# Low weight parts behind narrow products, newest sums first, and a gate multiplication on VectorE, in a hybrid decoder block on one core

## The chip, the cores and the metric

The kernel runs on one core of a Trainium2 chip. The metric is the device time of one execution in microseconds. TensorE (PE in the views; PEld is its weight load), VectorE (DVE), ScalarE (ACT), GpSimd (POOL) and SyncE (SP, which issues the weight DMAs) work side by side, each through its own instruction queue, in the order of the program, and wait for each other by semaphores.

## The reference

One decoder layer over 256 tokens of width 2048 in float32: a SwiGLU feed-forward network (FFN) of width 5632, a mixer (differential attention, a causal convolution, two sigmoid gates), a second FFN, and a final norm.

```
def swiglu(h, w_gate, w_up, w_down):
    return (jax.nn.silu(h @ w_gate) * (h @ w_up)) @ w_down

x = x + 0.5 * swiglu(rms_norm(x, ffn1_norm_g[l]), ffn1_w_gate[l], ffn1_w_up[l], ffn1_w_down[l])
h = rms_norm(x, mix_norm_g[l])
z = h @ w_in[l]
q, k, v, glu_a, glu_b, gate_a, gate_c = jnp.split(z, splits, axis=-1)
...
merged = jax.nn.sigmoid(gate_a) * attn_branch + jax.nn.sigmoid(gate_c) * conv_branch
x = x + merged @ w_out[l]
x = x + 0.5 * swiglu(rms_norm(x, ffn2_norm_g[l]), ffn2_w_gate[l], ffn2_w_up[l], ffn2_w_down[l])
return rms_norm(x, final_norm_g)
```

## The kernel before

All large matrix products are made in a reduced float format from split operands: a float32 weight is the sum of a high part (`wh`, a copy rounded to the format) and a low part (`wl`, what the rounding left), and so is an activation. A product is high x high + high x low + low x high.

**Weights.** They come in units of 512 rows x 512 columns (1 MB, `KU` = 4 row tiles), in the order in which they are used, into three raw buffers. The class `Weights` splits each unit in two halves (`KH` = 2 row tiles): `high_to` issues the copy to `wh` on ScalarE (L94, six buffers), `low_to` the subtraction to `wl` on VectorE (L103, four buffers). When both low parts of a unit are issued, its raw buffer is given up and the DMA for the unit three further on is issued (L107, on SyncE). `next` is called once per half and hands out the two parts. It first runs `high_to` and `low_to` ahead, so the low parts of the next unit are issued where a unit begins. They wait until TensorE has used the buffers that they overwrite.

**Products.** `lin` makes 512 output columns for 256 tokens, in four column tiles `ct`, each in a PSUM bank of its own (five banks in rotation). For each unit there are 16 wide products (L331: high weights by the activation's high and low parts side by side, 512 columns) and 16 narrow ones (L335: low weights by the activation's high part, 256 columns). Even units run wide, then narrow; odd units, and the last one of a product, narrow, then wide. A product over 2048 rows has four units, so TensorE's list reads wide, narrow, narrow, wide, wide, and so on: stretches of 32 equal products, half from one unit and half from the next. While the last unit's wide products run, each finished column tile starts a flow, which takes it out of PSUM: `halves_sum` (a ScalarE copy `rh`, L392, and a VectorE addition, L394) and then what the product needs. In the FFN an `up` product multiplies by the gate (L424) and splits the result (L261 on ScalarE, L263 on VectorE); a `gate` product multiplies by `rstd` (L404, VectorE), applies Silu (L406, ScalarE) and multiplies by `rstd` again (L407, GpSimd). `lin_tok` is the other form of product, with the tokens as rows (L375 to L377).

**The order.** No scheduler decides it: the program is recorded as it is written. `tick` is called behind each column tile; it moves every open flow one step on and then the side jobs (attention, convolution, small loads), each at a rate of its own. A flow's `yield` ends a step.

**The start.** Nothing is loaded ahead, so the first product takes its first three units half by half (`halves`). Before each half, `start` makes two tiles of the normed activation `h` and issues the squares for the norm on GpSimd (L273, L275).

The FFN's `w_gate`, `w_up` and `w_down` are used in three groups of 4, 4 and 3 column blocks; each block is a `gate` and an `up` product.

Of the kernel before, what the change touches and what calls it, by code (L numbers as in the profile page):

```python
# [25 lines left out]
KU = 4  # L26
KH = 2
# [14 lines left out]
class Weights:  # L42
# [54 lines left out]
    def low_to(self, n):  # L97
        while self.nlow < min(n, len(self.units) * KU // KH):
# [6 lines left out]
            if k + KH == KU:  # L105
                del self.raw[u]
                self.load_to(u + 1 + self.raw_bufs)  # L107

    def next(self, held=0, early=True):


        i = self.i

        def ahead(bufs):
            n = i + bufs - held
            if self.extra and n > min(self.extra) and i <= max(self.extra):
                n = min(n + len(self.extra), max(self.extra) + 1 + bufs)
            return n

        if early:  # L120
            self.high_to(ahead(self.high_bufs))
        self.low_to(ahead(self.low_bufs))
        self.i += 1
        return self.highs.pop(i), self.lows.pop(i)

# [30 lines left out]
def block_kernel(  # L156
# [156 lines left out]

    def tick(n=1):

        for f in list(flows):
            if next(f, flows) is flows:
                flows.remove(f)
        side.tick(n)

    def lin(nk, xs, evac, before=None):

        ps = [psum.tile([P, CK], F32, name="ps_mm", tag="mm") for _ in range(4)]
        nu = nk // KU

        def high(ct, parts, kt, i):
            w = parts[i // KH][0][:, i % KH, ct * P:(ct + 1) * P]  # L330
            nc.tensor.matmul(ps[ct], lhsT=w, rhs=xs(kt + i), start=(kt + i == 0), stop=(kt + i == nk - 1))  # L331

        def low(ct, parts, kt, i):
            w = parts[i // KH][1][:, i % KH, ct * P:(ct + 1) * P]
            nc.tensor.matmul(ps[ct][:, T:2 * T], lhsT=w, rhs=xs(kt + i)[:, 0:T], start=False, stop=False)  # L335

        def halves(u):

            for h in range(KU // KH):
                before(u * (KU // KH) + h)  # L340
                parts = [W.next(early=False)]
                for i in range(KH):
                    for ct in range(4):
                        high(ct, parts, u * KU + h * KH, i)
                for ct in range(4):
                    for i in range(KH):
                        low(ct, parts, u * KU + h * KH, i)
                tick(4)

        for u in range(nu):  # L350
            last = u == nu - 1
            if before is not None and not last:
                halves(u)
                continue
            parts = []
            for h in range(KU // KH):
                if before is not None:
                    before(u * (KU // KH) + h)
                parts.append(W.next(held=h))
            for product in ((low, high) if last or u % 2 == 1 else (high, low)):  # L360
                for ct in range(4):
                    for i in range(KU):
                        product(ct, parts, u * KU, i)
                    if product is high:
                        if last:
                            flows.append(evac(ct, ps[ct]))
                        tick(1.4)
                    elif ct % 2 == 1:
                        tick(1.2)
# [28 lines left out]
    def ffn_up(h, rstd, grp, a, before=None, late=None):  # L398
        s_2 = None

        def pair_of(ci, s_t):
            def gate_act(ct):
                s = s_t[:, ct, :]
                nc.vector.tensor_tensor(s, s, rstd, ALU.mult)  # L404
                yield
                nc.scalar.activation(s, s, AF.Silu)  # L406
                nc.gpsimd.tensor_tensor(s, s, rstd, ALU.mult)  # L407

            def gate_evac(ct, ps):
                halves_sum(s_t[:, ct, :], ps)  # L410
                if late is None or ci > 0:
                    yield from gate_act(ct)
                else:
                    yield

            def gate_late():
                yield from late
                for ct in range(4):
                    yield from gate_act(ct)

            def up_evac(ct, ps):
                t = tmp()
                halves_sum(t, ps)
                nc.vector.tensor_tensor(t, t, s_t[:, ct, :], ALU.mult)  # L424
                yield
                yield from split(a(ci * 4 + ct), t)

            lin(KT, h, gate_evac, before if ci == 0 else None)
            if late is not None and ci == 0:
                side.add(gate_late(), 0.5)  # L430
            lin(KT, h, up_evac)

        for ci in range(len(grp)):
            if ci % 2 == 0:
                s_2 = big.tile([P, 2, 4, T], F32, name="s_t", tag="y")
            pair_of(ci, s_2[:, ci % 2])
# [31 lines left out]

    def start(u):
        if u == 0:  # L470
            W.ahead = 1
            split_x(0)
            W.split_first()
        if u < 7:
            split_x(2 * u + 2)
        else:
            W.ahead = 3

    loads = {}

# [550 lines left out]
```

## Time and profile before

| what | value |
| --- | --- |
| runs (median of 3) | 2100.95 us (2100.57 to 2101.76) |
| the profiled execution, its own time | 2100.18 us |
| its span in the profile | 2098.4 us |
| TensorE busy | 2065.3 us (98%) |
| TensorE weight load busy | 1775.8 us (85%) |
| VectorE busy | 1375.9 us (66%) |
| ScalarE busy | 1004.8 us (48%) |
| GpSimd busy | 190.6 us (9%) |
| granted TensorE clock, mean of the span | 0.997 of full speed |
| low parts, L103 on VectorE | 731 instructions, 883.3 us |
| high parts, L94 on ScalarE | 731 instructions, 742.8 us |

In the profile a busy share says how much of the span an engine had an instruction running. Matmuls overlap and their ends are modelled, so the start of one to the start of a later one is the better measure of what a stretch of products takes. An idle time stands with the instruction behind it, and the name after the arrow is what ended the wait.

### The profile page before, as it was taken

The page shows a single profiled execution, that of the slowest core. Times are in us where ns is not written, and L with a number is a line of the kernel's source. Part 1 is how long each engine was busy: PE and PEld are TensorE (multiplying, and loading weights), DVE is VectorE, ACT ScalarE, POOL GpSimd, SP SyncE. Part 2 cuts the span into 40 slices and gives each one's busy share as a digit, 9 for nine tenths or more (in the row PEclk, how much of TensorE's full clock was granted, in tenths as well). Part 3 has the DMA queues.
Part 4 walks back from the last instruction along what each step waited for, and adds up shares of the span by engine and source line. Part 5 has one row for each costly group of instructions (what it writes and reads, how often), then busy time and mean ns, then how long its engine had stood idle before and what let it go on. Part 6 is the DMA issues. An engine that isn't in the chain of part 4 may idle for free.

```text
span 2098.4 us, 28546 instructions
## 1 busy us (share of the span) xinstructions
PE 2065.3 (98%) x11230; PEld 1775.8 (85%) x11230; DVE 1375.9 (66%) x1915; ACT 1004.8 (48%) x1456; POOL 190.6 (9%) x227
## 2 busy tenths in 40 slices
PE   7999999999999999999999999999999999999998
PEld 6888888888888888888778888888888888888887
DVE  8565555665565785889888666665655655645565
ACT  6454344443344554445555744554443444434443
POOL 6201012110010110000000000100100001000011
PEclk9999999999999999999999999999999999999999
DMA  6645555566545545555545555554455555554553
GB/s 241 197 171 212 188 177 206 189 216 218 181 180 202 193 174 201 181 187 186 183 166 180 198 181 181 198 203 180 168 214 183 184 195 181 201 193 168 203 198 121
DMA packets 57735, 397.54 MB, mean 189 GB/s; under 512 B 6888, under 2 KB 6992, under 8 KB 10752
## 3 DMA queue, kind: packets, MB, share of 16 engines
q1 hardware_dynamic: 55872, 390.10, 52.2%
q0 software_dynamic: 1728, 5.61, 0.9%
q8 instruction: 88, 1.44, 0.3%
q14 instruction: 47, 0.39, 0.1%
HBM read 392.00 MB, written 3.68 MB: 189 GB/s over the span
## 4 chain that ended last, share of the span: by engine, by line
PE 88%; DVE 7%; ACT 2%; DMA 1%; issue 1%; SPq 0%; DVEq 0%; ACTq 0%
PE ps_mm L331 40%; PE ps_mm L335 21%; PE ps_mm L375 9%; PE ps_mm L376 9%; PE ps_mm L377 9%; DVE wl L103 3%; DVE t L394 2%; DVE t L424 1%; ACT rh L392 1%; DMA w<-in_ffn_w_gate_dram 1%; ACT a L261 1%; DMA w<-in_ffn_w_down_dram 1%; PE ps_s L718 0%; PE ps_o L763 0%; PE ps_tr L907 0%
## 5 line engine op out<-in xcount | busy, mean ns | idle before, releaser
L103 DVE TENSOR_TENSOR wl<-w,wh 128x1024 fp32r<-128x1024 f32 x731 | 883.3, 1248 | 484.2 <-ACT wh L94 239.9
L94 ACT ACTIVATE wh<-w 128x1024 fp32r<-128x1024 f32 x731 | 742.8, 1053 | 704.0 <-PE ps_mm L331 377.5
L331 PE MATMUL ps_mm<-h,wh 128*128 128x512 f32 x2816 | 665.2, 392 | 10.8 <-DVE h L258 10.8
L331 PEld LDWEIGHTS ps_mm<-h,wh 128*128 128x128 f32 x2816 | 523.0, 189 | 117.4 <-ACT wh L84 6.2
L335 PEld LDWEIGHTS ps_mm<-h,wl 128*128 128x128 f32 x2816 | 340.9, 188 | 25.4 <-DVE wl L103 18.1
L335 PE MATMUL ps_mm<-h,wl 128*128 128x256 f32 x2816 | 349.8, 279 | 11.2 <-DVE wl L103 11.2
L407 POOL TENSOR_TENSOR s_t<-s_t,rstd 128x256 f32<-128x256 f32 x88 | 82.7, 940 | 1158.8 <-ACT s_t L406 1158.8
L331 PE MATMUL ps_mm<-a,wh 128*128 128x512 f32 x704 | 164.9, 390 | 0.4 <-DVE t L394 0.4
L331 PEld LDWEIGHTS ps_mm<-a,wh 128*128 128x128 f32 x704 | 130.4, 188 | 26.9 <-DVE t L394 0.8
L392 ACT ACTIVATE rh<-ps_mm 128x256 f32<-128x256 f32 x208 | 77.3, 372 | 153.7 <-PE ps_mm L331 153.7
L375 PE MATMUL ps_mm<-wl,a 128*128 128x512 f32 (+1 forms) x344 | 133.1, 387 | 0.0
L377 PE MATMUL ps_mm<-wh,a 128*128 128x512 f32 (+1 forms) x344 | 132.1, 384 | 0.0
L376 PE MATMUL ps_mm<-wh,a 128*128 128x512 f32 (+1 forms) x344 | 131.9, 384 | 0.0
L375 PE MATMUL ps_mm<-wl,hm 128*128 128x512 f32 x320 | 129.8, 406 | 0.0
L377 PE MATMUL ps_mm<-wh,hm 128*128 128x512 f32 x320 | 125.1, 391 | 0.0
L376 PE MATMUL ps_mm<-wh,hm 128*128 128x512 f32 x320 | 124.9, 390 | 0.0
L331 PE MATMUL ps_mm<-hm,wh 128*128 128x512 f32 x512 | 121.0, 392 | 0.0
L331 PEld LDWEIGHTS ps_mm<-hm,wh 128*128 128x128 f32 x512 | 94.7, 188 | 19.1
L619 DVE SCALAR_TENSOR_TENSOR y_sb<-u_sb,cw_sb,y_sb 128x256 f32<-128x256 f32 x240 | 105.0, 478 | 0.0
L394 DVE TENSOR_TENSOR t<-ps_mm,rh 128x256 f32<-128x256 f32 x112 | 47.5, 424 | 63.1 <-ACT rh L392 62.9
L335 PEld LDWEIGHTS ps_mm<-a,wl 128*128 128x128 f32 x704 | 84.5, 188 | 4.5 <-DVE wl L103 2.7
L335 PE MATMUL ps_mm<-a,wl 128*128 128x256 f32 x704 | 85.6, 278 | 1.9 <-DVE wl L103 1.9
(194 smaller groups left out, 1708.2 us busy)
## 6 DMA issues: line engine op xcount, KB each, us to landing
w<-in_ffn_w_up_dram SPq DMA_DIRECT2D x88, 1024.0 KB, 4.9
w<-in_ffn_w_down_dram SPq DMA_DIRECT2D x88, 1024.0 KB, 4.9
w<-in_ffn_w_gate_dram SPq DMA_DIRECT2D x85, 1024.0 KB, 4.9
w<-in_w_in_dram SPq DMA_DIRECT2D x72, 1024.0 KB, 4.8
w<-in_w_out_dram SPq DMA_DIRECT2D x16, 1024.0 KB, 4.9
w<-in_w_attn_branch_dram SPq DMA_DIRECT2D x8, 1024.0 KB, 4.8
w<-in_w_conv_branch_dram SPq DMA_DIRECT2D x8, 1024.0 KB, 4.8
w<-in_ffn_w_gate_dram SPq DMA_DIRECT2D x5, 512.0 KB, 8.5
```

Of the source, the lines that this page charges most:

```text
L94: self.nc.scalar.activation(wh, self.raw[u][:, k:k + KH], AF.Copy)
L103: self.nc.vector.tensor_tensor(wl, self.raw[u][:, k:k + KH], self.highs[h].bitcast(F32), ALU.subtract)
L261: nc.scalar.activation(dst[:, 0:T], src, AF.Copy)
L331: nc.tensor.matmul(ps[ct], lhsT=w, rhs=xs(kt + i), start=(kt + i == 0), stop=(kt + i == nk - 1))
L335: nc.tensor.matmul(ps[ct][:, T:2 * T], lhsT=w, rhs=xs(kt + i)[:, 0:T], start=False, stop=False)
L375: nc.tensor.matmul(ps, lhsT=hi, rhs=wl[:, kk, :], start=(first and kk == 0), stop=False)
L376: nc.tensor.matmul(ps, lhsT=hi, rhs=wh[:, kk, :], start=False, stop=False)
L377: nc.tensor.matmul(ps, lhsT=lo, rhs=wh[:, kk, :], start=False, stop=(last and kk == KH - 1))
L392: nc.scalar.activation(r, ps[:, T:2 * T], AF.Copy, scale=scale)
L394: nc.vector.tensor_tensor(dst, ps[:, 0:T], r, ALU.add)
L407: nc.gpsimd.tensor_tensor(s, s, rstd, ALU.mult)
L619: nc.vector.scalar_tensor_tensor(y, src, w, y, ALU.mult, ALU.add)
```

## The change

It has four parts. `tick` steps the open flows newest first. `next` no longer issues low parts in the start's halves beyond the next one (`i + 2`). In units that run narrow, then wide, `lin` calls the new `more_lows` twice: ahead of the wide products and behind the second column tile. It issues one and then a second low part for the unit after the next. And the gates' second multiplication by `rstd` goes from GpSimd to VectorE, one step later. `W.ahead` was set and not read.

```diff
+    def more_lows(self, n):
+
+        self.low_to(self.i + self.low_bufs - KU // KH + n)
...
         if early:
             self.high_to(ahead(self.high_bufs))
-        self.low_to(ahead(self.low_bufs))
+            self.low_to(ahead(self.low_bufs))
+        else:
+            self.low_to(i + 2)
         self.i += 1
         return self.highs.pop(i), self.lows.pop(i)
...
     def tick(n=1):
 
-        for f in list(flows):
+
+        for f in flows[::-1]:
             if next(f, flows) is flows:
                 flows.remove(f)
         side.tick(n)
...
                 parts.append(W.next(held=h))
-            for product in ((low, high) if last or u % 2 == 1 else (high, low)):
+            order = (low, high) if last or u % 2 == 1 else (high, low)
+            for product in order:
+                if product is high and order[0] is low:
+                    W.more_lows(1)
                 for ct in range(4):
+                    if product is high and order[0] is low and ct == 2:
+                        W.more_lows(2)
                     for i in range(KU):
                         product(ct, parts, u * KU, i)
...
                 nc.scalar.activation(s, s, AF.Silu)
-                nc.gpsimd.tensor_tensor(s, s, rstd, ALU.mult)
+                yield
+                nc.vector.tensor_tensor(s, s, rstd, ALU.mult)
...
     def start(u):
         if u == 0:
-            W.ahead = 1
             split_x(0)
             W.split_first()
         if u < 7:
             split_x(2 * u + 2)
-        else:
-            W.ahead = 3
```

TensorE's and SyncE's queues hold the same instructions in the same order as before. In the new kernel the lines have other numbers: 394 is 406, 404 is 416, 424 is 437, 263 is 269 (all VectorE), 392 is 404, 261 is 267 and 406 is 418 (ScalarE); 420 is the new multiplication.

VectorE's queue at the end of the first `up` product, before: sums, multiplications and splits of the four column tiles, and a pair of low parts.

```order
L394 TENSOR_TENSOR t_580<-ps_mm_397,rh_581 128x256
L424 TENSOR_TENSOR t_580<-t_580,s_t_118 128x256
L394 TENSOR_TENSOR t_590<-ps_mm_398,rh_591 128x256
L424 TENSOR_TENSOR t_590<-t_590,s_t_118 128x256
L263 TENSOR_TENSOR a1_0_116<-t_580,a1_0_116 128x256
L394 TENSOR_TENSOR t_601<-ps_mm_399,rh_602 128x256
L424 TENSOR_TENSOR t_601<-t_601,s_t_118 128x256
L263 TENSOR_TENSOR a1_0_116<-t_590,a1_0_116 128x256
L394 TENSOR_TENSOR t_612<-ps_mm_400,rh_613 128x256
L424 TENSOR_TENSOR t_612<-t_612,s_t_118 128x256
L103 TENSOR_TENSOR wl_625<-w_460,wh_550 128x1024
L103 TENSOR_TENSOR wl_627<-w_460,wh_552 128x1024
```

The same place now, from the first low part that belongs to it:

```order
L103 TENSOR_TENSOR wl_576<-w_460,wh_548 128x1024
L406 TENSOR_TENSOR t_582<-ps_mm_403,rh_583 128x256
L437 TENSOR_TENSOR t_582<-t_582,s_t_118 128x256
L406 TENSOR_TENSOR t_591<-ps_mm_404,rh_592 128x256
L437 TENSOR_TENSOR t_591<-t_591,s_t_118 128x256
L103 TENSOR_TENSOR wl_597<-w_460,wh_550 128x1024
L406 TENSOR_TENSOR t_605<-ps_mm_405,rh_606 128x256
L437 TENSOR_TENSOR t_605<-t_605,s_t_118 128x256
L269 TENSOR_TENSOR a1_0_116<-t_582,a1_0_116 128x256
L406 TENSOR_TENSOR t_616<-ps_mm_406,rh_617 128x256
L437 TENSOR_TENSOR t_616<-t_616,s_t_118 128x256
L269 TENSOR_TENSOR a1_0_116<-t_591,a1_0_116 128x256
```

The first low part of the pair (`wl_576`) now stands ahead of the first sum and the second (`wl_597`) behind the second; the splits into `a1` come later.

ScalarE's queue at the same place, before (`rh` is the copy out of PSUM, `a` the high part of the result):

```order
L392 ACTIVATE rh<-ps_mm 128x256
L261 ACTIVATE a_0_116<-t 128x256
L392 ACTIVATE rh<-ps_mm 128x256
L261 ACTIVATE a_0_116<-t 128x256
L392 ACTIVATE rh<-ps_mm 128x256
L261 ACTIVATE a_0_116<-t 128x256
L392 ACTIVATE rh<-ps_mm 128x256
L94 ACTIVATE wh<-w 128x1024 x2
L261 ACTIVATE a_0_116<-t 128x256
```

Now:

```order
L404 ACTIVATE rh<-ps_mm 128x256 x2
L267 ACTIVATE a_0_116<-t 128x256
L404 ACTIVATE rh<-ps_mm 128x256
L267 ACTIVATE a_0_116<-t 128x256
L404 ACTIVATE rh<-ps_mm 128x256
L267 ACTIVATE a_0_116<-t 128x256
L94 ACTIVATE wh<-w 128x1024 x2
L267 ACTIVATE a_0_116<-t 128x256
```

The second `rh` stands ahead of the first `a`, and so on to the end of the product.

VectorE's queue at the start, before (`h1` are the pairs of activation tiles, `w_84`, `w_90` and `w_95` the first three units):

```order
L258 SCALAR_TENSOR_TENSOR h1_0_110<-xT_82,g1_sb_80,h1_0_110 128x256 x2
L85 TENSOR_TENSOR wl_132<-w_84,wh_131 128x512 x2
L258 SCALAR_TENSOR_TENSOR h1_0_110<-xT_82,g1_sb_80,h1_0_110 128x256 x2
L103 TENSOR_TENSOR wl_149<-w_84,wh_147 128x1024
L103 TENSOR_TENSOR wl_155<-w_90,wh_153 128x1024
L103 TENSOR_TENSOR wl_159<-w_90,wh_157 128x1024
L258 SCALAR_TENSOR_TENSOR h1_0_110<-xT_82,g1_sb_80,h1_0_110 128x256 x2
L103 TENSOR_TENSOR wl_191<-w_95,wh_189 128x1024
L258 SCALAR_TENSOR_TENSOR h1_0_110<-xT_82,g1_sb_80,h1_0_110 128x256 x2
L103 TENSOR_TENSOR wl_221<-w_95,wh_219 128x1024
L258 SCALAR_TENSOR_TENSOR h1_1_111<-xT_82,g1_sb_80,h1_1_111 128x256 x2
```

Now:

```order
L264 SCALAR_TENSOR_TENSOR h1_0_110<-xT_82,g1_sb_80,h1_0_110 128x256 x2
L85 TENSOR_TENSOR wl_132<-w_84,wh_131 128x512 x2
L264 SCALAR_TENSOR_TENSOR h1_0_110<-xT_82,g1_sb_80,h1_0_110 128x256 x2
L103 TENSOR_TENSOR wl_149<-w_84,wh_147 128x1024
L264 SCALAR_TENSOR_TENSOR h1_0_110<-xT_82,g1_sb_80,h1_0_110 128x256 x2
L103 TENSOR_TENSOR wl_181<-w_90,wh_179 128x1024
L264 SCALAR_TENSOR_TENSOR h1_0_110<-xT_82,g1_sb_80,h1_0_110 128x256 x2
L103 TENSOR_TENSOR wl_211<-w_90,wh_209 128x1024
L264 SCALAR_TENSOR_TENSOR h1_1_111<-xT_82,g1_sb_80,h1_1_111 128x256 x2
L103 TENSOR_TENSOR wl_243<-w_95,wh_241 128x1024
L264 SCALAR_TENSOR_TENSOR h1_1_111<-xT_82,g1_sb_80,h1_1_111 128x256 x2
L103 TENSOR_TENSOR wl_273<-w_95,wh_271 128x1024
```

The two low parts of the second unit no longer stand ahead of the second half's `h1` pair; there is one low part between two pairs.

GpSimd's queue where the table of attention biases is made and sent out, before:

```order
L512 COPY bias_row<-tab_sb 8x12
L512 COPY bias_row<-tab_sb 8x14
L512 COPY bias_row<-tab_sb 8x143
L515 DMA row_114<-bias_row 8x384
L519 DMA spread<-row_114 128x768
L407 TENSOR_TENSOR s_t<-s_t,rstd_113 128x256 x2
L519 DMA spread<-row_114 128x768
L407 TENSOR_TENSOR s_t<-s_t,rstd_113 128x256 x2
L519 DMA spread<-row_114 128x768 x2
L523 DMA row_d<-spread 128x2x384 x4
L407 TENSOR_TENSOR s_t<-s_t,rstd_113 128x256 x12
L275 TENSOR_TENSOR acc_m<-acc_m,t 128x256 x15
```

Now:

```order
L522 COPY bias_row<-tab_sb 8x12
L522 COPY bias_row<-tab_sb 8x14
L522 COPY bias_row<-tab_sb 8x143
L525 DMA row_114<-bias_row 8x384
L529 DMA spread<-row_114 128x768 x4
L533 DMA row_d<-spread 128x2x384 x4
L281 TENSOR_TENSOR acc_m<-acc_m,t 128x256 x15
L589 MEMSET u_sb 128x8x30
```

The multiplications between the bias rows' copies and DMAs are gone.

## Rows read from the trace of the kernel before

**Rows 1.** The page: busy time, share and instructions of each engine.
```profile
PE 2065.3 (98%) x11230; PEld 1775.8 (85%) x11230; DVE 1375.9 (66%) x1915; ACT 1004.8 (48%) x1456; POOL 190.6 (9%) x227
```
**Rows 2.** List of waits: who waited for whom, total us, times, longest.
```profile
PEld ps_mm L335 <- DVE wl L103: 22.0, 41, 0.8
...
PE ps_mm L335 <- DVE wl L103: 13.9, 41, 0.6
```
**Rows 3.** TensorE's timeline, 52 to 91 us: start, us, instruction, count, idle before.
```profile
52.77 3.82 PE L335 MATMUL ps_mm<-h,wl 128*128 128x256 f32 x32
56.43 7.44 PE L331 MATMUL ps_mm<-h,wh 128*128 128x512 f32 x32
63.71 2.23 PE L335 MATMUL ps_mm<-h,wl 128*128 128x256 f32 x18
66.45 1.90 PE L335 MATMUL ps_mm<-h,wl 128*128 128x256 f32 x14 [0.51 <-DVE wl L103]
68.18 7.44 PE L331 MATMUL ps_mm<-h,wh 128*128 128x512 f32 x32
...
86.39 2.23 PE L335 MATMUL ps_mm<-h,wl 128*128 128x256 f32 x18
...
90.54 7.48 PE L331 MATMUL ps_mm<-h,wh 128*128 128x512 f32 x32
```
**Rows 4.** TensorE's timeline at the last stretch of either kind.
```profile
1937.61 2.23 PE L335 MATMUL ps_mm<-h,wl 128*128 128x256 f32 x18
...
1942.05 1.33 PE L331 MATMUL ps_mm<-h,wh 128*128 128x512 f32 x5
...
2005.74 2.23 PE L335 MATMUL ps_mm<-h,wl 128*128 128x256 f32 x18
...
2009.90 1.32 PE L331 MATMUL ps_mm<-h,wh 128*128 128x512 f32 x5
```
**Rows 5.** ScalarE's timeline, 53 to 60 us.
```profile
53.42 2.00 ACT L94 ACTIVATE wh<-w 128x1024 fp32r<-128x1024 f32 x2
57.55 0.38 ACT L392 ACTIVATE rh<-ps_mm 128x256 f32<-128x256 f32 x1 [2.14 <-PE ps_mm L331]
59.03 0.42 ACT L261 ACTIVATE a<-t 128x256 fp32r<-128x256 f32 x1 [1.09 <-DVE t L424]
```
**Rows 6.** VectorE's timeline, 54 to 67 us.
```profile
54.64 2.36 DVE L103 TENSOR_TENSOR wl<-w,wh 128x1024 fp32r<-128x1024 f32 x2 [1.58 <-ACT wh L94]
58.04 0.42 DVE L394 TENSOR_TENSOR t<-ps_mm,rh 128x256 f32<-128x256 f32 x1 [1.03 <-ACT rh L392]
...
59.75 0.42 DVE L394 TENSOR_TENSOR t<-ps_mm,rh 128x256 f32<-128x256 f32 x1 [0.76 <-ACT rh L392]
...
64.04 2.35 DVE L103 TENSOR_TENSOR wl<-w,wh 128x1024 fp32r<-128x1024 f32 x2
```
**Rows 7.** Timelines of TensorE, VectorE and GpSimd, 16 to 40 us.
```profile
17.63 3.78 PE L331 MATMUL ps_mm<-h,wh 128*128 128x512 f32 x8 [4.46 <-DVE h L258]
...
34.69 5.06 PE L331 MATMUL ps_mm<-h,wh 128*128 128x512 f32 x21 [0.25 <-DVE h L258]
39.59 0.59 PE L296 MATMUL ps_mean<-acc,ones 128*128 128x256 f32 x2
...
16.75 1.69 DVE L258 SCALAR_TENSOR_TENSOR h<-xT,g_sb,h 128x256 fp32r<-128x256 f32 x2
...
32.93 1.71 DVE L258 SCALAR_TENSOR_TENSOR h<-xT,g_sb,h 128x256 fp32r<-128x256 f32 x2
...
36.86 0.73 POOL L275 TENSOR_TENSOR acc<-acc,t 128x256 f32<-128x256 f32 x1
```
**Rows 8.** The page's DMA issues (median to landing), and the chain near 450 us.
```profile
w<-in_ffn_w_down_dram SPq DMA_DIRECT2D x88, 1024.0 KB, 4.9
...
449.25 10.55 DMA w<-in_ffn_w_down_dram
```
**Rows 9.** Groups of instructions: busy us, mean ns, idle before.
```profile
L404 DVE TENSOR_TENSOR s_t<-s_t,rstd 128x256 f32<-128x256 f32 x88 | 37.7, 431 | 2.9
```

## The prediction, made before the changed kernel had run

> **What bounds the kernel now.** I read the page first. TensorE counts as busy for 98% of the span [rows 1], and the work between its first and last product is the same before and after: the change gives TensorE the same list of instructions in the same order. So time can only come out of the places where TensorE waits. The second view is therefore the list of waits, and in it the reader should look for TensorE alone: nearly all its waits outside the first 40 us are one kind, a narrow product (L335) that waits for its low part `wl` from VectorE (L103), 41 times [rows 2].
>
> The third view, TensorE's timeline, shows what one of them costs. A stretch of 32 narrow products takes 3.66 us undisturbed: it starts at 52.77 and the wide ones follow at 56.43. The next stretch starts at 63.71 and is followed at 68.18, so it takes 4.47, which is 0.81 more [rows 3]. It breaks after 18 products, that is after 16 of the old unit and 2 of the new one: the second half of the second unit's low parts is what is missing. This stretch comes behind an `up` product. The one behind a `gate` product, 86.39 to 90.54, is 0.49 longer than 3.66 [rows 3]. In the timeline of the whole span I find 20 stretches of the first kind and 20 of the second. The last of each kind lose 0.78 (1937.61 to 1942.05) and 0.50 (2005.74 to 2009.90) [rows 4]. Three of the long kind run longer still; I count them at the price of the rest.
>
> Why the low part is late is in the timelines of ScalarE and VectorE around 58 us. At the end of a product four column tiles come out of PSUM, each by `rh` on ScalarE, an add, a multiplication and a split. ScalarE takes them oldest flow first: `rh` of tile 0 at 57.55, then `a` of tile 0, which waits 1.09 us for VectorE's multiplication and starts at 59.03, and `rh` of tile 1 only behind it [rows 5]. So VectorE's adds come at 58.04 and 59.75, 1.71 apart [rows 6], while TensorE finishes a tile every 0.91 us (a quarter of 16 wide products, and 32 of them go from 56.43 to 63.71, 7.28 us) [rows 3]. Behind the fourth tile, at 64.04, stands the pair of low parts that TensorE needs, 2.35 us long [rows 6]. It ends at 66.39, and TensorE goes on at 66.45 [rows 3].
>
> **The change part by part.** *Low parts behind narrow products.* In every second unit, and in the last of each product, the two low parts for the unit after next are now issued behind that unit's narrow products, one ahead of the wide ones and one after two column tiles. I replay the place at 63.71. The last unit's narrow products end when its wide ones start, at 56.43 [rows 3]. That frees the first buffer; its high part is there, since ScalarE's pair began at 53.42 and took 2.00 [rows 5]. So the first low part runs from 56.43 to about 57.6 (half of 2.36) [rows 6], before the first add at 58.04. The second stands behind the add and multiplication of tiles 0 and 1.
>
> *Newest sum first.* `rh` of tile 1 now stands ahead of `a` of tile 0. TensorE has tile 1 done 0.91 after tile 0, so `rh` comes at 57.55 + 0.91 = 58.46, the add at about 58.95, the multiplication ends near 59.85, and the second low part is done near 61.0. It is needed for the 19th product of a stretch that starts at 63.71, near 65.8: 4.8 us to spare. What is now ahead of the late low part, two tiles, was four. I see nothing left that could make TensorE wait there, so the whole excess of the stretch goes: 20 x 0.79 (mean of 0.81 and 0.78) = 15.9, and 20 x 0.50 = 9.9, together 25.8 us.
>
> Here a rule of the Trainium skill bears on the reading. TensorE's own idle time in these waits is 13.9 us, the weight load's 22.0 [rows 2], and the stretches are 25.8 longer. The Trainium skill, page "Trainium Kernel Development and Optimization", section "Performance Expectations", calls matmul busy time a bad measure of how close a kernel is to its roofline, because matmuls are pipelined. By idle time alone the first two parts would give 13.9, and the time would be about 2086; the starts of the stretches speak for the larger sum, and the trace so agrees with the page.
>
> *The gates' second multiplication on VectorE.* 88 instructions leave GpSimd. The first multiplication by the same `rstd`, on the same tile, takes 431 ns on VectorE [rows 9], so 88 x 0.43 = 38 us more there. VectorE has the room: its share was two thirds [rows 1]. In the `gate` products three of the four stand behind all four sums, and the new instruction waits for ScalarE's Silu. Queued behind it are the low parts of the unit after next, needed more than 7 us later, since a whole wide stretch (7.28) lies between. I cost it at 0 on the path. It could cost up to the short kind's 0.5 in each of 20 products, if a wait for Silu reached the next stretch (9.9); a gain on the path is excluded, because no one waits for GpSimd's result for long: it is read a whole product later.
>
> *The start.* The first three units now make one low part per half instead of three ahead. In VectorE's queue two low parts leave the front of the pairs of `h`. TensorE's pause before 17.63 was a wait for `h`, 4.46 us [rows 7], and that pair of `h` started at 16.75 behind two low parts of unit 1. Its own input is there earlier, so this pause nearly goes. But from there VectorE sets the pace: from 16.75 to 32.93 five pairs of `h` and five low parts take 16.18 us, 3.2 per half [rows 7]. The last pair of `h` moves up by two low parts, some 3.3, to about 29.6; behind it now stands a low part that TensorE needs before the last unit's remaining 14 narrow and 16 wide products (14 x 0.114 + 16 x 0.228 = 5.2). That ends near 36.6. Before, the wide products of that unit end 13 products after 34.69, near 37.7 [rows 7]. Gain about 1.0. Bounds: above, the mean's matmul at 39.59 needs GpSimd's last add, which ends at 36.86 + 0.73 = 37.6 [rows 7], so no more than 2.0. Below, the eight wide products behind the pause took 3.78 us, 1.96 more than eight at 0.228 [rows 7]; if such a slow stretch stays and meets the path, the start loses 2.0 instead.
>
> *GpSimd's queue.* Without the multiplications, which waited for ScalarE, GpSimd's queue no longer has anything that holds back the bias rows and their DMAs. They ran near 450 us, where a load of weights took 10.55 us instead of 4.9 [rows 8]; now they come in the first hundred microseconds. The collision moves, it does not grow: 0 in my sum. Bounds: it could cost its excess of 5.65 once where loads have less lead, or cost nothing where it costs something now (a gain of up to 1.5, two stretches' worth).
>
> The sum: 25.8 + 0 + 1.0 + 0 = 26.8 us. The profiled execution took 2100.18, so 2073.4; the median of the runs is 0.77 above that, so 2074.2, and I say 2074.
>
> **The rivals.** (a) *The short kind stays.* The gate ends have four more VectorE instructions, each behind a Silu. If that eats what the order gives there, 9.9 of the 26.8 stays: 2084. For it: the chain add, multiply, Silu, multiply goes twice between two engines. Against: both low parts are issued ahead of all but one of these multiplications.
>
> (b) *The waits are renamed.* If the low parts come late because of the high parts or the loads, they are not earlier for being issued earlier; then only the start moves and the time is 2100. Against: the high pair ended at 55.42, 8 us before the stretch [rows 5].
>
> (c) *Slower: the PSUM bank.* The second low part now stands in front of the sums of tiles 2 and 3. A product takes four of five banks, so the next product's fourth column tile writes the bank of tile 2. It starts at 56.43 + 28 x 0.228 = 62.8; by the replay the sum of tile 2 ends at about 61.5. That is 1.3 us to spare. There are 44 FFN products that end so. To lose all of 26.8 each would have to be 0.6 over, so the sum 1.9 us later than I work out, which is where slower begins; at 2.5 us late the time is 2074 + 44 x 1.2 = 2127. The profile speaks against it: nothing of that length is in VectorE's queue at this place but the low part I have counted.
>
> (d) *The loads.* The moved DMAs find the loads with less lead: up to 5.65 more, 2080.
>
> **How the numbers follow.** The forecast, all 40 stretches undisturbed, has 0.78; it spans 2069.5 (start and collision at their good ends, three long stretches gone whole) to 2077. (a) 0.08, (d) 0.05, (b) 0.04, (c) 0.05. A difference of 0.2%, 4.2 us, is about what a measurement of this kernel can tell from none. Faster: 0.78 + 0.08 + 0.05 = 0.91. Same: 0.04. Slower: 0.05. The range takes in the forecast and (d) and most of (a): 2069.5 to 2083; what lies outside holds under 2 in 10.
>
> **What would show it.** In the list of waits, TensorE's line for `wl` L103 should be nearly gone, below 2 us from 13.9. In the timelines each 32 narrow products should take 3.66, at about 62 and 84 us too. VectorE's adds at a product's end should be about 1 us apart for tiles 0 and 1, with a low part between tiles 1 and 2. TensorE's first pause, 4.46, should be under 1 us. GpSimd's bias rows should run before 100 us. I am wrong if TensorE waits for an add (L406 of the new kernel), or if the waits for `wl` stay at half their number.

## The result

The changed kernel takes 2072.81 us (median of 4 runs, 2072.36 to 2073.36), the kernel before 2101.34 beside it (4 runs). The ratio is 0.9865, with a 95% interval of 0.9848 to 0.9882: faster by 1.35%. The forecast was 2074. The profiled execution of after took 2073.36 with a span of 2071.5; that of before 2100.18 and 2098.4, so the span is 26.9 us shorter and the sum had said 26.8. That the two agree to 0.1 us is luck: the sum's term for the body of the kernel was 2.4 us too small and its term for the start 2.3 us too large.

### The profile page after: what moved, and what is told of

The parts are those of the page before. It is cut to its first block, busy times and chain, and to the rows that moved or that the text cites. A ratio compares the mean times of both kernels' runs of the same rounds, so it can differ in the third digit from the quotient of the medians.

```text
span 2071.5 us, 28470 instructions
## 1 busy us (share of the span) xinstructions
PE 2051.5 (99%) x11230; PEld 1771.1 (85%) x11230; DVE 1379.7 (67%) x2003; ACT 1019.6 (49%) x1456; POOL 102.5 (5%) x139
## 4 chain that ended last, share of the span: by engine, by line
PE 98%; DVE 1%; DMA 0%; issue 0%; ACT 0%; SPq 0%; ACTq 0%; DVEq 0%
PE ps_mm L338 47%; PE ps_mm L342 24%; PE ps_mm L387 9%; PE ps_mm L388 9%; PE ps_mm L389 9%; DMA w<-in_ffn_w_gate_dram 0%; PE ps_s L728 0%; DVE wl L103 0%; DVE h L264 0%; PE ps_o L773 0%; PE ps_mg L881 0%; PE ps_tr L917 0%; PE ps_at L763 0%; PE ps_mean L302 0%; PE ps_tr L816 0%
## 5 line engine op out<-in xcount | busy, mean ns | idle before, releaser
L103 DVE TENSOR_TENSOR wl<-w,wh 128x1024 fp32r<-128x1024 f32 x731 | 872.9, 1230 | 562.9 <-ACT wh L94 377.4
L338 PE MATMUL ps_mm<-h,wh 128*128 128x512 f32 x2816 | 663.1, 392 | 6.4 <-ACT wh L84 5.7
L338 PEld LDWEIGHTS ps_mm<-h,wh 128*128 128x128 f32 x2816 | 522.8, 188 | 111.3 <-ACT wh L84 5.7
L342 PE MATMUL ps_mm<-h,wl 128*128 128x256 f32 x2816 | 339.9, 278 | 5.1 <-DVE wl L103 5.0
L338 PE MATMUL ps_mm<-a,wh 128*128 128x512 f32 x704 | 164.6, 390 | 0.0
L338 PEld LDWEIGHTS ps_mm<-a,wh 128*128 128x128 f32 x704 | 130.4, 188 | 26.1
L338 PE MATMUL ps_mm<-hm,wh 128*128 128x512 f32 x512 | 120.9, 391 | 0.0
L338 PEld LDWEIGHTS ps_mm<-hm,wh 128*128 128x128 f32 x512 | 94.8, 188 | 19.1
L389 PEld LDWEIGHTS ps_mm<-wh,a 128*128 128x128 f32 x344 | 64.5, 187 | 13.9
L387 PEld LDWEIGHTS ps_mm<-wl,a 128*128 128x128 f32 x344 | 64.6, 188 | 13.0
```

What stands on the lines that cost most here:

```text
L103: self.nc.vector.tensor_tensor(wl, self.raw[u][:, k:k + KH], self.highs[h].bitcast(F32), ALU.subtract)
L387: nc.tensor.matmul(ps, lhsT=hi, rhs=wl[:, kk, :], start=(first and kk == 0), stop=False)
L389: nc.tensor.matmul(ps, lhsT=lo, rhs=wh[:, kk, :], start=False, stop=(last and kk == KH - 1))
```

## The profile after

The page's row of engines answers to [rows 1].

```profile
PE 2051.5 (99%) x11230; PEld 1771.1 (85%) x11230; DVE 1379.7 (67%) x2003; ACT 1019.6 (49%) x1456; POOL 102.5 (5%) x139
```

The list of waits of TensorE and of its weight load (who waited for whom: total us, times, longest) answers to [rows 2].

```profile
PE ps_mm L338 <- ACT wh L84: 5.7, 1, 5.7
PE ps_mm L342 <- DVE wl L103: 5.0, 3, 2.8
...
PEld ps_mm L342 <- DVE wl L103: 6.4, 4, 3.0
```

TensorE (PE) waits for `wl` 3 times where it was 41, and these three are new ones, in the first 32 us. With 5.0 us they miss the sign "below 2 us" that the forecast had set. The timeline of TensorE of after (start, us, instruction, count, idle before) answers to [rows 3].

```profile
54.06 3.82 PE L342 MATMUL ps_mm<-h,wl 128*128 128x256 f32 x32
57.71 7.44 PE L338 MATMUL ps_mm<-h,wh 128*128 128x512 f32 x32
64.99 3.82 PE L342 MATMUL ps_mm<-h,wl 128*128 128x256 f32 x32
68.64 7.44 PE L338 MATMUL ps_mm<-h,wh 128*128 128x512 f32 x32
...
86.86 3.82 PE L342 MATMUL ps_mm<-h,wl 128*128 128x256 f32 x32
90.51 1.78 PE L338 MATMUL ps_mm<-h,wh 128*128 128x512 f32 x7
```

Each stretch of 32 narrow products is one unbroken row, and the wide ones follow after 3.65 us, behind an `up` product (64.99) and behind a `gate` product (86.86) alike. VectorE and ScalarE of after at the same product's end answer to [rows 5, 6].

```profile
58.84 0.39 ACT L404 ACTIVATE rh<-ps_mm 128x256 f32<-128x256 f32 x1 [2.14 <-PE ps_mm L338]
59.75 0.38 ACT L404 ACTIVATE rh<-ps_mm 128x256 f32<-128x256 f32 x1 [0.52 <-PE ps_mm L338]
60.63 0.42 ACT L267 ACTIVATE a<-t 128x256 fp32r<-128x256 f32 x1 [0.50 <-DVE t L437]
...
58.59 1.21 DVE L103 TENSOR_TENSOR wl<-w,wh 128x1024 fp32r<-128x1024 f32 x1
59.73 0.41 DVE L406 TENSOR_TENSOR t<-ps_mm,rh 128x256 f32<-128x256 f32 x1
60.17 0.43 DVE L437 TENSOR_TENSOR t<-t,s_t 128x256 f32<-128x256 f32 x1
60.52 0.42 DVE L406 TENSOR_TENSOR t<-ps_mm,rh 128x256 f32<-128x256 f32 x1
60.97 0.42 DVE L437 TENSOR_TENSOR t<-t,s_t 128x256 f32<-128x256 f32 x1
61.31 1.22 DVE L103 TENSOR_TENSOR wl<-w,wh 128x1024 fp32r<-128x1024 f32 x1
62.45 0.42 DVE L406 TENSOR_TENSOR t<-ps_mm,rh 128x256 f32<-128x256 f32 x1
```

The second `rh` comes 0.91 after the first, ahead of any `a`; the sums of tiles 0 and 1 are 0.79 apart (before: 1.71); the two low parts stand ahead of tile 0 and between tiles 1 and 2. The second one is done at 62.53 and is needed at 64.99 + 18 x 0.114 = 67.04.

The start is the place where time was lost. The timelines of TensorE and, last, of VectorE answer to [rows 7].

```profile
13.77 2.08 PE L338 MATMUL ps_mm<-h,wh 128*128 128x512 f32 x8 [0.72 <-ACT wh L94]
...
28.03 0.50 PE L342 MATMUL ps_mm<-h,wl 128*128 128x256 f32 x2 [1.98 <-DVE wl L103]
31.32 3.36 PE L342 MATMUL ps_mm<-h,wl 128*128 128x256 f32 x14 [2.79 <-DVE wl L103]
34.47 6.56 PE L338 MATMUL ps_mm<-h,wh 128*128 128x512 f32 x24
40.87 0.59 PE L302 MATMUL ps_mean<-acc,ones 128*128 128x256 f32 x2
...
29.52 6.51 DVE L103 TENSOR_TENSOR wl<-w,wh 128x1024 fp32r<-128x1024 f32 x4
```

Three windows of after there: from and to, length, busy time and count of TensorE, its weight load, VectorE, ScalarE and GpSimd, then granted clock, DMA share, GB/s.

```profile
24.00:28.00 4.00, 1.80 (x11) 1.16 (x9) 4.00 (x5) 2.94 (x3) 3.84 (x4) 1.00 0.56 174
28.00:32.00 4.00, 1.18 (x5) 0.98 (x6) 4.00 (x4) 2.01 (x2) 3.84 (x5) 0.70 0.22 94
32.00:36.00 4.00, 4.00 (x17) 3.71 (x17) 4.00 (x3) 0.00 (x0) 3.92 (x3) 0.50 1.01 297
```

The pause of 4.46 has become 0.72, as forecast. But the last unit now waits 1.98 and 2.79 us for low parts, the granted clock falls to 0.50 (1.2 GHz) behind these pauses, and the 14 narrow products take 3.15 us to the next row where 14 x 0.114 = 1.6 had been counted. The mean's matmul comes at 40.87, 1.28 later than before. No other profiled execution with this start has it as late; the section on the prediction compares them.

## Experiments: one part alone

The working theory was that a low part arrived 0.6 us late (66.39, where the 19th product was due at 63.71 + 18 x 0.114 = 65.76), and that anything that moves it forward by that much gives the whole gain. The rival was that each part brings its own share. Every kernel here was timed beside the kernel before.

**e1_newest: the order of the sums alone.**

```diff
-        for f in list(flows):
+        for f in flows[::-1]:
```

> The kernel before with the newest-first order of the flows alone. Theory one (either of the two orders is enough by itself): with the sums 0.91 us apart the four tiles are through VectorE near 62.3 in the stretch that starts at 63.71, the pair of low parts behind them ends near 64.7, and it is needed near 65.5; so the 40 stretches lose nothing and the time is about 2074 (28 below the kernel before, no loss at the start). Theory two (the two orders add, each brings about half): about 2088. Theory three (the early low parts do the work alone): 2100.

2072.07 us (2071.14 to 2072.22), ratio 0.9863 [0.9848, 0.9878]: the whole gain. VectorE and TensorE of this kernel at the end of the same `up` product:

```profile
61.78 2.35 DVE L103 TENSOR_TENSOR wl<-w,wh 128x1024 fp32r<-128x1024 f32 x2
...
63.29 3.82 PE L335 MATMUL ps_mm<-h,wl 128*128 128x256 f32 x32
```

The pair of low parts still stands behind all four sums, but begins at 61.78 in place of 64.04 and ends at 64.13. It is needed at 63.29 + 2.05 = 65.34, so 1.2 us are to spare.

**e2_lows: the low parts behind the narrow products alone.** The sums stay oldest first.

```diff
+            order = (low, high) if last or u % 2 == 1 else (high, low)
+            for product in order:
+                if product is high and order[0] is low:
+                    W.more_lows(1)
...
+                    if product is high and order[0] is low and ct == 2:
+                        W.more_lows(2)
```

> The kernel before with the low parts behind the narrow products alone; sums still oldest first. Theory one: the pair is done near 62 where 65.5 would do, so the stretches lose nothing; but the second low part now pushes the third sum to end near 62.7, and the bank that it empties is needed at 62.8, so waits of up to 0.2 us may come in their place: 2073 to 2080. Theory two (the orders add): about 2088. Theory three (the order of the sums does the work alone): 2100.

2074.01 us (2073.97 to 2074.43), 0.9874 [0.9859, 0.9888]: nearly the whole gain again. No stretch waits for `wl` any more. What is left over is seen in its list of waits.

```profile
PE ps_mm L335 <- DVE xT L451: 0.7, 3, 0.3
PE ps_mm L335 <- DVE t L403: 0.4, 1, 0.4
```

The last of these in TensorE's timeline:

```profile
456.57 1.19 PE L335 MATMUL ps_mm<-a,wh 128*128 128x512 f32 x4 [0.39 <-DVE t L403]
```

These are wide products that wait for a sum behind three column tiles: the PSUM bank of rival (c), though at a few places only. e1_newest and the changed kernel do not have these waits.

**e3_mult: the gates' second multiplication on VectorE alone.**

```diff
-                nc.gpsimd.tensor_tensor(s, s, rstd, ALU.mult)
+                yield
+                nc.vector.tensor_tensor(s, s, rstd, ALU.mult)
```

> The kernel before with the gates' second multiplication on VectorE alone. Theory one: at a gate product's end two of the four new multiplications (0.43 us each) come ahead of the late pair of low parts, so the 20 short stretches lose some 0.8 us more each: about 2117. Rival (VectorE's room hides it, as the prediction put it at 0): 2101. If the shared queue is not what counts but GpSimd's use of memory beside VectorE, it would be a little faster, 2098.

2099.5 us (2096.82 to 2100.58, 10 runs), 0.9992 [0.9983, 1.0001]. My 2117 was a miss, and the trace shows three things behind the number. VectorE of e3_mult at the end of a `gate` product, in order of time:

```profile
129.28 0.42 DVE L394 TENSOR_TENSOR s_t<-ps_mm,rh 128x256 f32<-128x256 f32 x1 [0.76 <-ACT rh L392]
129.74 0.42 DVE L404 TENSOR_TENSOR s_t<-s_t,rstd 128x256 f32<-128x256 f32 x1
130.08 0.42 DVE L408 TENSOR_TENSOR s_t<-s_t,rstd 128x256 f32<-128x256 f32 x1
130.92 0.42 DVE L394 TENSOR_TENSOR s_t<-ps_mm,rh 128x256 f32<-128x256 f32 x1 [0.42 <-ACT rh L392]
```

First, VectorE stood idle 0.76 us ahead of each sum, waiting for `rh`; the added multiplication (L408) falls into that hole, which shrinks to 0.42, and the sums stay 1.64 apart. I had added its 0.42 to the path. Second, at the ends of `up` products the stretch loses 0.50 in place of 0.78. VectorE's product with `s_t` no longer reads what GpSimd wrote. The groups of that instruction, before and after (busy us, mean ns | idle before):

```profile
L424 DVE TENSOR_TENSOR t<-t,s_t 128x256 f32<-128x256 f32 x88 | 37.5, 426 | 9.5 <-DVE t L394 0.5
```

```profile
L437 DVE TENSOR_TENSOR t<-t,s_t 128x256 f32<-128x256 f32 x88 | 37.4, 426 | 3.0
```

The second line is that of the changed kernel; e3_mult's own, L425, has the same 3.0. The idle time ahead of it falls from 9.5 to 3.0 us for 88, 0.07 each; four of these stand in front of the low parts, 0.28 together, and about 20 x 0.28 = 5.6 us come back. Third, 5.8 us are lost elsewhere: 2.0 near 86 us, where ScalarE waits 3.30 us for a load of `up` weights beside the bias rows' transfers, which now run there, and 3.8 near 1370 us, for which see e7_late_lows.

**e4_start: the new start alone.**

```diff
         if early:
             self.high_to(ahead(self.high_bufs))
-        self.low_to(ahead(self.low_bufs))
+            self.low_to(ahead(self.low_bufs))
+        else:
+            self.low_to(i + 2)
```

> The kernel before with the start's shorter look ahead alone. The changed kernel's matmul for the mean began at 40.87 where it was 39.59 before, so theory one (this part alone lost the start) expects 1.3 us slower, 2102.6, with two pauses of TensorE of 2 and 2.8 us behind 26 us. The prediction's replay expected 1.0 faster, 2100.3. If the loss at the start came from another part, 2101.3.

2101.1 us (2100.57 to 2102.92), 1.0004 [0.9995, 1.0014]: no difference. The pauses of 2.09 and 2.66 us in front of the last unit's narrow products are there too, and the mean's matmul is at 39.99, 0.40 later than before.

## Experiments: one part undone

Each is the changed kernel with one part put back as it was.

**e5_old_start.**

```diff
-            self.low_to(ahead(self.low_bufs))
-        else:
-            self.low_to(i + 2)
+        self.low_to(ahead(self.low_bufs))
```

> The changed kernel with the start's low parts as they were before (always the full look ahead). Theory: it gives back the 1.3 us that the start lost: 2071.5 against 2072.8. Rival (the start's loss is the clock and comes whatever the order): 2072.8.

2071.73 us (2071.64 to 2072.48), 0.9867 [0.9853, 0.9882]: 1.1 under after by the medians, but no difference by the ratios, since the kernel before was faster too beside it (2099.76). The mean's matmul is at 39.16 here.

**e6_oldest.**

```diff
-        for f in flows[::-1]:
+        for f in list(flows):
```

> The changed kernel with the flows stepped oldest first again. Theory one (either order is enough): the low parts are early still; the third sum is late, at the edge of its bank's need: 2073 to 2082. Theory two (they add): about 2087.

2075.05 us (2074.26 to 2076.76), 0.9883 [0.9869, 0.9898]. The stretches are whole, and the waits of e2_lows are back (`PE ps_mm L338 <- DVE xT L455: 0.8, 3, 0.3` in its list): each of the three costs about 0.5 us from start to start, and so does one wait for a sum near 1362 us (L406). From the mean's matmul to the end the trace has 2032.9 us where after has 2030.6, so these four are 2.0 of 2.3.

**e7_late_lows.**

```diff
-                if product is high and order[0] is low:
-                    W.more_lows(1)
...
-                    if product is high and order[0] is low and ct == 2:
-                        W.more_lows(2)
```

> The changed kernel with the low parts back where a unit begins, the rest as changed. Theory one: the newest-first sums are through in time even with two of the gates' multiplications ahead of the pair: 2073 to 2075. Theory two (they add): about 2087.

2076.62 us (2075.27 to 2077.21), 0.9889 [0.9874, 0.9904]: 3.8 over after, and 4.5 over e1_newest, which issues its low parts just as late. All the stretches but one are whole. The one, with the work on VectorE and GpSimd around it:

```profile
1351.05 2.23 PE L342 MATMUL ps_mm<-h,wl 128*128 128x256 f32 x18
1355.20 2.90 PE L342 MATMUL ps_mm<-h,wl 128*128 128x256 f32 x14 [1.92 <-DVE wl L103]
...
1349.34 5.81 DVE L103 TENSOR_TENSOR wl<-w,wh 128x1024 fp32r<-128x1024 f32 x2
...
1340.95 0.55 POOL L907 DMA_DIRECT2D fg<-in_final_norm_g_dram  x1
1349.92 5.87 POOL L945 TENSOR_SCALAR fg<-fg 128x2048 f32<-128x2048 f32 x1 [8.42 <-DMA fg<-in_final_norm_g_dram]
```

TensorE waits for a low part, the second of a pair. VectorE begins it at 1350.47, without a wait, and it takes 4.67 us where the first took 1.22: beside it GpSimd scales `fg`, the final norm's row, whose transfer of 1 MB it had issued 10 us earlier. The expectation of y7_pool, next, puts the loss down to that transfer and to a load of `up` weights that is late beside it. But the high part that waits for this load (2.37 us, from 1351.57) belongs to the next pair of low parts, which starts at 1356.32. The narrow products take 6.85 us to the next row where 3.65 is the rule, and the wide ones behind them 0.63 more than 7.28, in a window (1356 to 1360) with a granted clock of 0.60: 3.8 together. In e3_mult the same subtraction takes 4.67 us beside the same scaling, near 1370 us.

**y7_pool: e7_late_lows with the multiplication back on GpSimd.**

```diff
-                yield
-                nc.vector.tensor_tensor(s, s, rstd, ALU.mult)
+                nc.gpsimd.tensor_tensor(s, s, rstd, ALU.mult)
```

> The kernel e7_late_lows with the second multiplication back on GpSimd (that is newest sum first and the new start, nothing else). Theory one: what e7_late_lows lost against the changed kernel is a collision. Its trace has GpSimd's 1 MB transfer for the final norm (fg) issued at 1340.95, beside the load of the first up weights; that load's high part starts only at 1351.57 and TensorE loses 3.6 us near 1352. With the multiplication on GpSimd the transfer stands in the queue behind four multiplications and is issued some 20 us later (1363 in e1_newest), so the loss is gone: about 2073.0. Theory two: the low parts that are issued late are themselves the cause: the time stays at 2076.6 and TensorE waits for wl near 1352 as in e7_late_lows.

2072.5 us (2071.35 to 2073.5), 0.9867 [0.9851, 0.9884]: the 4.1 us are back. GpSimd and TensorE of this kernel at the same place:

```profile
1362.74 1.58 POOL L414 TENSOR_TENSOR s_t<-s_t,rstd 128x256 f32<-128x256 f32 x1 [1.25 <-ACT s_t L413]
1364.26 0.57 POOL L906 DMA_DIRECT2D fg<-in_final_norm_g_dram  x1
...
1351.01 3.82 PE L342 MATMUL ps_mm<-h,wl 128*128 128x256 f32 x32
```

The multiplications, which wait for ScalarE, had held the transfer back in GpSimd's queue by some 23 us, and the scaling until 1979.54. The pair of low parts that begins at 1349.30 here takes 2.35 us. One other stretch loses 1.0, at 456.81, behind a late load, with the bias rows' transfers again just ahead of it (432 to 444 us). In the changed kernel the scaling runs early too:

```profile
1347.73 5.50 POOL L950 TENSOR_SCALAR fg<-fg 128x2048 f32<-128x2048 f32 x1 [4.44 <-DMA fg<-in_final_norm_g_dram]
```

Nothing is lost there, since the low parts are issued earlier: one ends at 1347.99, the next begins at 1353.75, and what runs beside the scaling is the norm's chain (L293 takes 2.02 us in place of 0.43). So two parts of the change are linked: one brings a collision of GpSimd's work with VectorE's, the other covers it.

**e8_pool: the changed kernel with the multiplication back on GpSimd** (the same edit).

> The changed kernel with the gates' second multiplication back on GpSimd. Theory: beside the new order it costs and brings nothing on the path: 2072.8, with GpSimd's bias rows and their DMAs near 450 us again; at most 1.5 us slower if that collision costs there what it did before. Rival (the move to VectorE is a part of the gain): 2078 or more.

2072.28 us (2071.91 to 2072.43), 0.9869 [0.9853, 0.9886]: the same as after.

## Experiments: the start, and the edge of the bank

**s2_half_end: the first product's last unit taken half by half.** In that unit alone the loops are turned, and the late gate's side work starts four ticks later.

```diff
+        for h in range(KU // KH):
+            for product in (low, high):
...
+                for ct in range(4):
...
+                    for i in range(h * KH, (h + 1) * KH):
+                        product(ct, parts, u * KU, i)
...
-                side.add(gate_late(), 0.5)
+                side.add(gate_late(), 0.5, delay=4)
```

> Start from the changed kernel; only the last unit of the very first product is taken half by half (narrow, wide, narrow, wide) in place of all narrow products and then all wide ones, and the late gate's side work begins four ticks later. Theory one: the start of the changed kernel lost time because TensorE stood in front of narrow products whose low parts VectorE makes last (pauses of 1.98 and 2.79 us at 26 to 31 us, and a granted clock of 0.5 behind them); with eight wide products to do meanwhile the pauses shrink, the mean's matmul comes at about 38.1 in place of 40.87 (GpSimd's last add, ending near 38.0, is next), and the time is 2.5 us under the changed kernel's 2072.8, so about 2070.3. Theory two: VectorE's low parts set the end of the start whatever TensorE does in between; the mean's matmul stays at 40 to 41 and the time at 2072 to 2073.

2070.37 us (2070.16 to 2071.07), 0.9858 [0.9842, 0.9875], 2.4 under after by the medians, 1.5 by the ratios: the time as theory one had it, and the fastest kernel here. That is less than the 0.2% that I count as measurable, but the runs don't overlap and the trace shows the place. TensorE's timeline of s2_half_end:

```profile
27.82 1.20 PE L359 MATMUL ps_mm<-h,wl 128*128 128x256 f32 x8 [1.98 <-DVE wl L103]
...
36.25 3.43 PE L355 MATMUL ps_mm<-h,wh 128*128 128x512 f32 x12 [1.12 <-DVE s_t L426]
...
61.95 3.82 PE L359 MATMUL ps_mm<-h,wl 128*128 128x256 f32 x32
```

Its window from 32 to 36 us, with the columns as above:

```profile
32.00:36.00 4.00, 3.12 (x15) 2.25 (x14) 4.00 (x4) 1.15 (x3) 3.92 (x3) 1.00 1.03 299
```

Of the two pauses one is left, and the clock stays at 1.00. The stretch that stood at 64.99 begins at 61.95, 3.0 earlier than in after, whose start is the slowest of its kind, and 1.3 earlier than in the fastest of them (63.21, y7_pool). My detail was wrong: the mean's matmul comes at 40.43 and not 38.1, because it now stands later among the products; and TensorE waits 1.12 for a sum, which is next in line.

**x1_spare and x3_spare: VectorE's work at a product's end made longer.** Behind each FFN sum VectorE does one, or three, multiplications that nobody reads (`spare` is 1 or 3).

```diff
+        for _ in range(spare):
+            nc.vector.tensor_tensor(r, r, r, ALU.mult)
```

> Start from the changed kernel; behind each FFN sum VectorE does one spare multiplication of the right half by itself (0.42 us, read by nobody), 176 in all, 74 us of VectorE time. Theory one (the low parts and the PSUM bank of tile 2 have room): in the changed kernel the sum of tile 2 ends 1.56 us before the next product's fourth column tile writes its bank (1954.57 against 1949.76 + 28 x 0.2275 = 1956.13); two spare instructions ahead of it push it by at most 0.9, the second low part is needed still later, so the time stays at 2072 to 2074. Theory two (VectorE's work at a product's end is on the path, at its own price): 176 x 0.34 = 60 us, so about 2130.

2073.1 us (2072.39 to 2073.69), 0.987 [0.9855, 0.9885]: 176 instructions more, 74 us of VectorE time, and no difference from after. The sum of tile 2, the one that empties the bank of rival (c), starts 0.63 us later behind its product than in after.

> The same with three spare multiplications behind each FFN sum. They push the sum of tile 2 by about 2 x 1.13 = 2.25 us, 0.7 us past the moment at which the next product's fourth column tile needs the bank. Theory one (the PSUM bank decides once its 1.56 us are used up): TensorE waits for a sum about 0.7 us in each of some 40 FFN products, 28 us, so about 2100, and the list of waits names the sums, not the low parts. Theory two (there is no such edge; the low parts or nothing at all decide): the time stays below 2080, or TensorE's waits are for the low parts.

2122.86 us (2122.36 to 2123.35, 2 runs), 1.0107 [1.0087, 1.0127]: slower than the kernel before. Its list of waits:

```profile
PE ps_mm L338 <- DVE s_t L406: 16.5, 21, 1.0
PE ps_mm L338 <- DVE t L406: 16.0, 19, 2.0
```

TensorE and, last, VectorE at one end of an `up` product:

```profile
1951.50 6.54 PE L338 MATMUL ps_mm<-h,wh 128*128 128x512 f32 x28
1958.83 1.20 PE L338 MATMUL ps_mm<-h,wh 128*128 128x512 f32 x4 [0.80 <-DVE t L406]
1959.87 3.79 PE L342 MATMUL ps_mm<-h,wl 128*128 128x256 f32 x32
...
1958.36 0.41 DVE L406 TENSOR_TENSOR t<-ps_mm,rh 128x256 f32<-128x256 f32 x1
```

The wait is for sums, 40 times, and it breaks the wide products after 28, where the fourth column tile begins. That is the edge that rival (c) named. The sum of tile 2 starts 6.86 behind the product (1951.50), 4.39 in after, so 2.47 later and not 2.25; the 32 products take 8.37 in place of 7.28, 1.09 each time and not 0.7. There are 37 such rows in the trace, 1.09 to 1.24 us each, and they make 41 of the 50 us; another 5.9 are at the first `up` product's end, near 70 us, where TensorE falls behind.

## Why the prediction was right, and where it was not

*What bounds the kernel, and the 40 stretches: right.* From the mean's matmul to the end the trace of before has 2098.4 - 39.59 = 2058.8 us, that of after 2071.5 - 40.87 = 2030.6: 28.2 less, where 25.8 had been counted. The term was too small because I took the three longer stretches at the price of the rest. Measured from start to start they had lost 1.59, 0.99 and 1.14; all 40 together come to 27.2, and the last 1.0 is mostly a wait of wide products near 466 us, beside the bias rows' transfers, which have moved.

*Idle time against starts.* The waits for `wl` of [rows 2] count 13.9 us of idle TensorE, and nearly all of them are gone; the body of the kernel became 28.2 shorter. The same 11230 products count 2051.5 us of busy time now and 2065.3 before, so about half of the loss had been booked as work. What the Trainium skill says in "Trainium Kernel Development and Optimization", section "Performance Expectations", that matmul busy time is a bad measure of how close a kernel is to its roofline because matmuls are pipelined, is borne out here: idle time would have given 2086.

*The two orders: the mechanism right, the division of labour not seen.* The replay gave sums about 1 us apart and the second low part near 61.0; corrected for the later start of after (57.71 in place of 56.43) that is 62.3, and it was 62.53. But I told the two edits as if both were needed for 4.8 us of room. The part was 0.6 late, and each edit alone moves it by more than that (e1_newest, e2_lows). The second brings room, not time.

*The multiplication: 0, right* (e8_pool against after). Rival (a), which let it eat the short kind's gain, is out. That it took a wait of 0.07 off each product with `s_t` I had not seen; it is worth about 5.6 us to the kernel before and nothing once the low parts are early.

*The start: wrong, and in sign.* The forecast was a gain of 1.0; after's profile has a loss of 1.28. That is the largest of its kind: in the eight profiled executions with the new start the mean's matmul comes at 39.09 (y7_pool) to 40.87 (after), 40.07 on average, and in the five with the old one at 39.09 to 39.82, 39.37 on average. So the new start loses about 0.7 us, with a spread wider than that, and the times of e4_start and e5_old_start do not resolve it. The failed step is "14 x 0.114 + 16 x 0.228 = 5.2": it priced the products behind the pauses at full clock. From 31.32 to the mean's matmul they took 9.55 us with eight more wide products (1.8), so 2.5 too many; in the other seven executions they took 8.5 to 9.4, so part of the loss hangs on when the clock recovers. My lower bound had said where such a slow stretch could appear, but I took it as the less likely case. Nor does the 36.6 follow from its own terms. A pair of `h` from 29.6 (1.7 us) and the low part behind it (1.6) would put the end near 38.1, which is no gain. That the products could begin at 31.32, as 36.6 implies, is luck: the last pair of `h` came at 27.90.

*GpSimd's queue: 0 in the sum, right for a reason that I gave only half.* The bias rows' transfers now run near 60 to 72 us and cost TensorE nothing. In e3_mult, where both orders are the old ones, they cost 2.0 there; that is the mechanism of rival (d), a load with less lead. I had not followed the queue as far as `fg`. e7_late_lows and y7_pool price its scaling, beside a low part, at 4.1 us, and the early low parts cover that too.

*Rival (b)* is out: the low parts were late because of their place in the queue. *Rival (c)* is real as a mechanism; the edge lies about 1.4 us (2.47 less 1.09) from where the changed kernel stands.

## What to carry to other kernels

Before adding up the parts of a change, ask how late the late thing is: two edits that each cure a lateness of 0.6 us give one gain, and the second buys room only. An engine that waits ahead of every step of a chain can take more work there for nothing, up to an edge at which another resource (here the PSUM bank of an earlier tile) takes all of it at once; find the edge by adding dummy work. And work that is taken off a queue also releases what stood behind it: follow that queue to its end, transfers and the work that waits for them included.

## What the runs showed of the hardware that was not expected

TensorE's clock in the start: behind pauses of 1.98 and 2.79 us it was granted 0.50 from 32 to 36 us, and a stretch counted at 1.6 us took 3.15. With the pauses broken up (s2_half_end) the same window shows 1.00. In before, the same happened behind the pause of 4.46 (0.50 and 0.65 from 16 to 24 us). In all eight profiled executions with the new start it falls there; the lowest of their windows shows 0.50 to 0.76.

GpSimd beside VectorE: in eight of the traces GpSimd's scaling of `fg` (128x2048, 5.4 to 6.3 us) meets a low part, and that one takes 4.2 to 4.7 us where 1.22 is the rule. In the kernel before this happens near 2010 us and costs TensorE nothing; in e3_mult and e7_late_lows TensorE waits for just that part. The gates' first multiplication has a mean of 460 ns in e8_pool, where GpSimd multiplies the same tiles in between, and 425 in after, where it doesn't; in the start of after, beside GpSimd's adds, a low part takes 1.63 us where it takes 1.22 later on. The Trainium skill, "GPSIMD Engine Reference", section "8. Key points", says that the two share their SBUF interfaces and contend when a VectorE instruction has two SBUF inputs; these numbers agree. Not every such instruction is slowed: in after, L294 takes its 0.43 us within the scaling.

A VectorE product that reads what GpSimd finished long before starts 0.07 us later than the same product of VectorE's own results (L424 against L437 above, 88 each).
